# The first norm of a hybrid decoder step, its squares taken from a second load of x and applied within the fourth tile

## The chip, the core and the metric

The kernel runs on one core of one Trainium2 chip. The metric is device time in microseconds (us) for one execution; the times below are medians of three runs, and one further execution was profiled.

## The reference, cut to what matters

One layer of a decoder trunk is computed for 512 prompt tokens and 32 sample tokens (8 sequences of 4). The part concerned is its beginning: the first RMSNorm and the input projection.

```python
def rmsnorm(x, w):
    xf = x.astype(jnp.float32)
    y = xf * lax.rsqrt(jnp.mean(xf * xf, axis=-1, keepdims=True) + EPS)
    return (y * w.astype(jnp.float32)).astype(x.dtype)
...
    h = rmsnorm(x, norm_mix_w)
    proj = h @ w_in
    ...
    xbc = proj[..., o4:o5]
    dt_raw = proj[..., o5:]
    ...
    xbc_c, new_conv_ssd = causal_dwconv(xbc, conv_ssd_prev, conv_ssd_w, conv_ssd_b)
    xbc_c = jax.nn.silu(xbc_c)
    ...
    dt = jax.nn.softplus(dt_raw.astype(f32) + dt_bias.astype(f32))
    ...
    y, ssm_new = ssd_scan(xs, dt, A, Bm, Cm, ssm_prev)
```

x has 2048 columns; `xbc` has 12 tiles of 128 columns (tiles 0 to 7 feed the scan's values, 8 and 9 its B, 10 and 11 its C), dt has 16 columns. Attention, the output projection and the gated MLP follow and take most of the time.

## The kernel before, in words

Activations lie transposed: 128 columns of x on the partitions, the 544 tokens in two halves of 272 (256 prompt, 16 sample). x has 16 such k-tiles. Each fp32 operand is split into a rounded part (`hi`) and a residual (`lo`), and a product is three matmuls, hi·hi, lo·hi and hi·lo (`mm3`, L166 on; every matmul is recorded at L158). The norm's factor `rstd` differs by token only, so the matmuls take x times the norm's weights, and `rstd` is multiplied in where a PSUM tile is read (the evictions at L305 and L306).

The start works as follows. For each k-tile of x (the loop over `k`): SyncE loads `xt` into one of six buffers (L241); for even k the next 256 columns of the weights of tiles 8 and 10 (`FIRST`) are loaded (L149) and split, `whi` by ScalarE (L150) and `wlo` by VectorE (L151), two raw buffers being shared by all weight loads; then x is split, `xh` by VectorE for even k (L251) and by ScalarE for odd k (L253), and `xl` by VectorE (L254). ScalarE squares `xt` (L257, L260); GpSimd, for every fourth k VectorE, adds the squares into `ssq` (L261). TensorE runs the two first tiles over all k together into four PSUM halves (three buffers of the tag `po`, one of `sB`); after the fourteenth k it multiplies `ones` by `ssq` and `rms_rstd` takes root and reciprocal. After these tiles comes dt's projection (`dt_linear`: 64 matmuls whose weights, `wdthi`, are split at L274 and L275). Then the evictions and convolutions of tiles 8 and 10, tiles 0 to 3, the other six tiles, and so on. `conv` evicts two halves, runs three multiply-adds on VectorE (L316) and SiLU on ScalarE.

What sets the order. TensorE's order is the order in which the program is written. On the other engines a scheduler orders the instructions: of those that its model calls ready, the earliest written goes first. Each queue (the five engines and SyncE's DMA queue) then runs strictly in its order. Work that is to be woven between the matmuls of the projections is written as tasks of the class `Side`: `mm3` calls `side.poll()`, and a task goes on when the matmul time since its last step exceeds what it yielded. dt's steps (`dt_stage`), lambda (`lam`) and the two groups of the scan (`ssd`) are such tasks, each starting after the one ahead of it. Weight tiles are loaded and split ahead of need: `plan` queues sources, `wfill(n)` issues splits until n chunks of 1024 columns wait in `wbuf`, and `wnext` fills up to three and takes one; the chunks rotate through three buffers each of `whi` and `wlo`.

Memory is given out in pools stacked by address. The pool `sA` (the buffers `xt`, `ssq`, `sq`, and four `whi` and four `wlo` of 4 KB per partition for the first tiles) is released after the first tiles' matmuls, and `sS` takes the same addresses: `mixy0`, `mixy1` (8.5 KB each), `ctail`, `bc0` to `bc3` (2.1 KB each), then what is asked for next. A tile of `sS` can be written only when the tile of `sA` under it has been read for the last time.

Of the kernel before, what the change touches and what calls it, by code (L numbers as in the profile page):

```python
# [16 lines left out]
P = 128  # L17
# [82 lines left out]
def body(tc, i, o):  # L100
# [32 lines left out]
    def half(tag="po"):  # L133
        return ps.tile([P, 512], F32, name="po", tag=tag, bufs=3 if tag == "po" else 1)
# [60 lines left out]
    def linear(xs, evac, tags=("po", "po")):  # L195

        ch = [wnext(), wnext()]
        for hf in range(2):
            po = half(tags[hf])
            for k in range(NK):  # L200
                mm3(po, kslice(ch, k), xs[k], hf, k == 0, k == NK - 1)
            evac(hf, po)

# [20 lines left out]
    xs = {}  # L224
    ssq = sA.tile([P, 2, HT], F32, name="ssq")
    ssq2 = sA.tile([P, 2, HT], F32, name="ssqb")
    first = [[half(), half()], [half(), half("sB")]]
# [9 lines left out]
    fw = [[], []]  # L237
    sub = 256
    for k in range(NK):
        xt = sA.tile([P, 2, HT], F32, name="xt", tag="xt", bufs=6)  # L240
# [8 lines left out]
        xs[k] = xslot(k)  # L249
        if k % 2 == 0:  # L250
            V.tensor_scalar(xs[k][0], xt, nw_mix[:, k:k + 1], None, op0=ALU.mult)  # L251
        else:
            A.activation(xs[k][0], xt, AF.Copy, scale=nw_mix[:, k:k + 1])  # L253
        V.scalar_tensor_tensor(xs[k][1], xt, nw_mix[:, k:k + 1], rd(xs[k][0]), op0=ALU.mult, op1=ALU.subtract)  # L254
        e, acc = (V, ssq2) if k % 4 == 2 else (G, ssq)
        if k in (0, 2):
            A.activation(acc, xt, AF.Square)  # L257
        else:
            sq = sA.tile([P, 2, HT], F32, name="sq", tag="sq", bufs=3)
            A.activation(sq, xt, AF.Square)  # L260
            e.tensor_tensor(acc, acc, sq, op=ALU.add)  # L261
    k1 = pack(cst, "k1")
    ones, nw_ffn, nw_fin = (k1[n] for n in ("ones", "nw_ffn", "nw_fin"))
    V.tensor_tensor(ssq, ssq, ssq2, op=ALU.add)
    kS = pack(sC, "kS")
# [6 lines left out]
    wdt = kS["w_dt"].rearrange("p (k h) -> p k h", h=SH)  # L272
    whi = sC.tile([P, NK, 2 * SH], FR, name="wdthi")
    A.activation(whi[:, :, 0:SH], wdt, AF.Copy)  # L274
    V.tensor_tensor(whi[:, :, SH:2 * SH], wdt, rd(whi)[:, :, 0:SH], op=ALU.subtract)  # L275
    for k in range(NK):
        for f in range(2):
            for hf in range(2):
                mm3(first[f][hf], kslice(fw[f], k), xs[k], hf, k == 0, k == NK - 1)
        if k == 13:  # L280
            rstd = rms_rstd(cst, ssq, DM, tag="rstd")
    sA.release()
# [5 lines left out]
    ctail = sS.tile([P, NC_X, 27], F32, name="ctail")  # L288
    bc = [sS.tile([P, 2, HT], F32, name=f"bc{j}") for j in range(4)]
    def conv(pool, tg, lin, nw, par, prev, tail, dst, bufs=2):  # L290

# [34 lines left out]
    def xbc(j):  # L326
        dst = mixy[j // 4][:, j % 4] if j < 8 else bc[j - 8]
        evac = conv(sS, "s", LX, CW, cpar[:, j], cprev[:, j], ctail[:, j], dst)
        if j in FIRST:
            for hf in range(2):  # L330
                evac(hf, first[FIRST.index(j)][hf])
        else:
            linear(xs, evac)
# [10 lines left out]
    def dt_stage(po, res):  # L344
        yield 1.5
        dtr = sS.tile([2 * SH, SEQ + NS3], F32, name="dtr", tag="spre", bufs=2)
# [273 lines left out]
    squared = []  # L620
    podt = dt_linear()
    res = []
    t_dt = side.add(dt_stage(podt, res))


# [25 lines left out]

    for j in FIRST:
        xbc(j)
    for j in range(4):
        xbc(j)
# [821 lines left out]
def host_inputs(x):  # L1477
# [5 lines left out]
    xx = np.concatenate([x["x_prompt"].reshape(SEQ, DM), x["x_sample"].reshape(NS, DM)], 0)[perm]  # L1483
    d["xT"] = xx.T.reshape(NK, P, 2, HT)
    w_in = np.asarray(x["w_in"])[0]
    nt = 44
# [123 lines left out]
```

## Time and profile before

| | |
|---|---|
| median of 3 runs | 2421.18 us (2420.86 to 2428.1) |
| profiled execution | 2424.79 us, of which the span of instructions is 2423.0 us |
| TensorE busy | 2349.6 us (97%), 18184 matmuls |
| VectorE busy | 2074.0 us (86%) |
| ScalarE busy | 1140.5 us (47%) |
| GpSimd busy | 677.1 us (28%) |
| DMA moved | 350.44 MB, 145 GB/s in the mean |

In the rows PE is TensorE's matmuls, PEld its weight loads, DVE VectorE, ACT ScalarE, POOL GpSimd, SP SyncE; a q behind an engine is its queue of DMA issues. L150 is a line of the kernel's file. Times are us from the start of the span, durations of one instruction in groups are ns. PEclk is the clock granted to TensorE, 1.00 being 2.4 GHz and 0.50 being 1.2 GHz. An arrow in brackets names what ended an idle time. Busy times of TensorE are modelled from pipelined matmuls, so its pace is better read from the starts of successive matmuls.

### The profile page before, as it was taken

The page shows a single profiled execution, that of the slowest core. Times are in us where ns is not written, and L with a number is a line of the kernel's source. Part 1 is how long each engine was busy: PE and PEld are TensorE (multiplying, and loading weights), DVE is VectorE, ACT ScalarE, POOL GpSimd, SP SyncE. Part 2 cuts the span into 40 slices and gives each one's busy share as a digit, 9 for nine tenths or more (in the row PEclk, how much of TensorE's full clock was granted, in tenths as well). Part 3 has the DMA queues.
Part 4 walks back from the last instruction along what each step waited for, and adds up shares of the span by engine and source line. Part 5 has one row for each costly group of instructions (what it writes and reads, how often), then busy time and mean ns, then how long its engine had stood idle before and what let it go on. Part 6 is the DMA issues. An engine that isn't in the chain of part 4 may idle for free.

```text
span 2423.0 us, 46336 instructions
## 1 busy us (share of the span) xinstructions
PE 2349.6 (97%) x18184; PEld 2299.1 (95%) x18184; DVE 2074.0 (86%) x2925; ACT 1140.5 (47%) x1651; POOL 677.1 (28%) x643
## 2 busy tenths in 40 slices
PE   7999999999999999899999999999999899899997
PEld 7989898998999999899999999999999899899997
DVE  8686778787876556999999999999999988988986
ACT  5645345656565333444444444444444534435345
POOL 4243233333321111233223232322222122222323
PEclk9999999999999999999999999999999999999998
DMA  4434444454544543333434343343433755747432
GB/s 157 139 119 137 154 155 144 143 160 147 164 161 155 167 137 120 120 127 123 137 111 138 119 142 119 128 133 115 139 109 132 228 179 176 228 153 249 124 114 83
DMA packets 172284, 350.44 MB, mean 145 GB/s; under 512 B 19474, under 2 KB 89874, under 8 KB 172066
## 3 DMA queue, kind: packets, MB, share of 16 engines
q1 hardware_dynamic: 168370, 335.51, 43.2%
q0 software_dynamic: 2880, 11.14, 1.3%
q8 instruction: 143, 2.34, 0.4%
q10 hardware_dynamic: 816, 0.84, 0.1%
q14 instruction: 75, 0.61, 0.1%
HBM read 293.07 MB, written 54.35 MB: 143 GB/s over the span
## 4 chain that ended last, share of the span: by engine, by line
PE 61%; DVE 6%; DMA 2%; ACT 1%; issue 1%; SPq 0%; DVEq 0%; ACTq 0%
PE po L158 59%; DVE wlo L1063 1%; DVE wx L1063 1%; DVE xl L1063 1%; DMA st<-hTs 1%; DMA st<-hB 1%; ACT whi L1069 1%; DVE ssq L1467 0%; DMA wraw<-in_w_last 0%; PE pos L158 0%; PE scs L158 0%; DVE acc L316 0%; DVE T2l L1063 0%; DVE y L1449 0%; DMA wraw<-in_w_down 0%
## 5 line engine op out<-in xcount | busy, mean ns | idle before, releaser
L158 PE MATMUL po<-xh,whi 128*128 128x272 f32 x3968 | 1159.8, 292 | 12.7 <-ACT whi L150 5.2
L158 PE MATMUL po<-xh,wlo 128*128 128x272 f32 x3968 | 1151.5, 290 | 6.2 <-DVE wlo L1063 5.0
L158 PE MATMUL po<-xl,whi 128*128 128x272 f32 x3968 | 1149.6, 290 | 6.5 <-DVE xl L254 6.5
L158 PEld LDWEIGHTS po<-xh,whi 128*128 128x128 f32 x3968 | 756.3, 191 | 20.8 <-ACT whi L150 5.2
L158 PEld LDWEIGHTS po<-xh,wlo 128*128 128x128 f32 x3968 | 754.5, 190 | 13.6 <-DVE wlo L1063 6.8
L158 PEld LDWEIGHTS po<-xl,whi 128*128 128x128 f32 x3968 | 754.8, 190 | 7.5 <-DVE xl L254 7.5
L1069 ACT ACTIVATE whi<-wx 128x1024 fp32r<-128x1024 f32 (+2 forms) x340 | 343.3, 1010 | 475.7 <-PE po L158 452.8
L1063 DVE TENSOR_TENSOR wlo<-wx,whi 128x1024 fp32r<-128x1024 f32 (+2 forms) x340 | 429.6, 1264 | 49.3 <-ACT whi L1069 47.0
L151 DVE TENSOR_TENSOR wlo<-wraw,whi 128x1024 fp32r<-128x1024 f32 (+1 forms) x132 | 167.2, 1272 | 61.7 <-ACT whi L150 61.4
L1069 ACT ACTIVATE whi<-wraw 128x1024 fp32r<-128x1024 f32 (+2 forms) x136 | 137.0, 1007 | 173.2 <-PE po L158 168.5
L150 ACT ACTIVATE whi<-wraw 128x1024 fp32r<-128x1024 f32 (+1 forms) x132 | 127.8, 976 | 101.5 <-PE po L158 72.1
L1063 DVE TENSOR_TENSOR wlo<-wraw,whi 128x1024 fp32r<-128x1024 f32 (+2 forms) x136 | 167.8, 1234 | 5.0 <-ACT whi L1069 2.7
L1063 DVE TENSOR_TENSOR wx<-wraw,wx 128x1024 f32<-128x1024 f32 (+2 forms) x136 | 166.2, 1222 | 1.2
L699 POOL TENSOR_TENSOR kvl<-kv,kvh 128x512 fp32r<-128x512 f32 x64 | 104.5, 1634 | 180.4 <-ACT kvh L697 167.3
L158 PE MATMUL po<-T1h,wlo 128*128 128x272 f32 x512 | 148.6, 290 | 5.8 <-DVE wlo L1063 5.8
L158 PE MATMUL po<-T2h,wlo 128*128 128x272 f32 x512 | 148.6, 290 | 5.0 <-DVE wlo L1063 5.0
L158 PE MATMUL po<-T2h,whi 128*128 128x272 f32 x512 | 147.9, 289 | 2.2 <-ACT whi L1069 2.2
L158 PE MATMUL po<-T1h,whi 128*128 128x272 f32 x512 | 147.7, 289 | 1.4 <-ACT whi L1069 1.4
L158 PE MATMUL po<-T2l,whi 128*128 128x272 f32 x512 | 148.1, 289 | 0.0
L158 PE MATMUL po<-T1l,whi 128*128 128x272 f32 x512 | 148.1, 289 | 0.0
L158 PE MATMUL po<-B11h,whi 128*128 128x272 f32 x512 | 147.1, 287 | 0.7 <-DVE u L1139 0.7
L158 PE MATMUL po<-B11h,wlo 128*128 128x272 f32 x512 | 147.6, 288 | 0.0
(408 smaller groups left out, 4155.3 us busy)
## 6 DMA issues: line engine op xcount, KB each, us to landing
wx<-in_w_gu SPq DMA_DIRECT2D x88, 512.0 KB, 3.9
wraw<-in_w_gu SPq DMA_DIRECT2D x88, 512.0 KB, 3.9
wraw<-in_w_in SPq DMA_DIRECT2D x84, 512.0 KB, 3.8
kv<-in_kc SPq DMA_DIRECT2D x128, 128.0 KB, 2.2
kv<-in_vc SPq DMA_DIRECT2D x128, 128.0 KB, 2.8
wraw<-in_w_out SPq DMA_DIRECT2D x32, 512.0 KB, 3.7
wx<-in_w_down SPq DMA_DIRECT2D x32, 448.0 KB, 3.9
wraw<-in_w_down SPq DMA_DIRECT2D x32, 448.0 KB, 3.7
```

Of the source, the lines that this page charges most:

```text
L150: A.activation(hi[:, c], raw[:, c], AF.Copy)
L151: V.tensor_tensor(lo[:, c], raw[:, c], rd(hi[:, c]), op=ALU.subtract)
L158: T.matmul(out, lhsT=lhsT, rhs=rhs, start=start, stop=stop)
L699: e.tensor_tensor(l[:, s], src[:, s], rd(h)[:, s], op=ALU.subtract)
L1063: e.tensor_tensor(out, a, b, op=op)
L1069: A.activation(h, src, AF.Copy)
```

## The change

The squares leave the split loop, with their accumulators and GpSimd's and VectorE's additions; ScalarE now makes all sixteen `xh`. ScalarE's order becomes the written order from the loop to the end of the norm (`manual_schedule`). x is loaded a second time with the tokens on the partitions (`xtp`, `xts`: ten pieces of up to 128 tokens x 1024 columns, 512 KB each but for two of 32 tokens), on ScalarE's own DMA queue, three buffers of the tag `m` in `sS` in turn. ScalarE squares each piece with a sum along the row. The first three issues are written behind the split loop, ahead of dt's weight split; the four PSUM halves of tiles 8 and 10 are copied to `bc` so that their buffers come free. TensorE goes on without the norm: dt, tile 0, the first half of tile 1. There `norm1` takes root and reciprocal by token, spreads them on diagonals (128 x 640) and multiplies with `ones`; then come the second half of tile 1, the evictions and convolutions of 0, 1, 8 and 10 and tiles 2 and 3. dt's task starts behind the norm, its first pause is gone.

```diff
--- before.py
+++ after.py
@@ -196,10 +196,14 @@
 
         ch = [wnext(), wnext()]
         for hf in range(2):
-            po = half(tags[hf])
-            for k in range(NK):
-                mm3(po, kslice(ch, k), xs[k], hf, k == 0, k == NK - 1)
-            evac(hf, po)
+            evac(hf, linear_half(ch, hf, tags[hf], xs))
+
+    def linear_half(ch, hf, tag, x=None):
+        x = x or xs
+        po = half(tag)
+        for k in range(NK):
+            mm3(po, kslice(ch, k), x[k], hf, k == 0, k == NK - 1)
+        return po
 
     def xslot(k):
         return [xsp.tile([P, 2, HT], FR, name=f"x{n}{k}", tag=f"x{n}{k}") for n in "hl"]
@@ -222,8 +226,6 @@
     sC = tc.alloc_tile_pool(name="sC", bufs=1)
     sA = tc.alloc_tile_pool(name="sA", bufs=1)
     xs = {}
-    ssq = sA.tile([P, 2, HT], F32, name="ssq")
-    ssq2 = sA.tile([P, 2, HT], F32, name="ssqb")
     first = [[half(), half()], [half(), half("sB")]]
     for j in list(range(4)) + [9, 11, 4, 5, 6, 7]:
         plan(i["w_in"][32 + j])
@@ -236,6 +238,8 @@
         plan(i["w_in"][28 + j])
     fw = [[], []]
     sub = 256
+    act = contextlib.ExitStack()
+    act.enter_context(tc.manual_schedule(engines={mybir.EngineType.Activation}))
     for k in range(NK):
         xt = sA.tile([P, 2, HT], F32, name="xt", tag="xt", bufs=6)
         dma(out=xt, in_=i["xT"][k])
@@ -247,21 +251,10 @@
             for c in ch:
                 c[2]((k % 8) // 2)
         xs[k] = xslot(k)
-        if k % 2 == 0:
-            V.tensor_scalar(xs[k][0], xt, nw_mix[:, k:k + 1], None, op0=ALU.mult)
-        else:
-            A.activation(xs[k][0], xt, AF.Copy, scale=nw_mix[:, k:k + 1])
+        A.activation(xs[k][0], xt, AF.Copy, scale=nw_mix[:, k:k + 1])
         V.scalar_tensor_tensor(xs[k][1], xt, nw_mix[:, k:k + 1], rd(xs[k][0]), op0=ALU.mult, op1=ALU.subtract)
-        e, acc = (V, ssq2) if k % 4 == 2 else (G, ssq)
-        if k in (0, 2):
-            A.activation(acc, xt, AF.Square)
-        else:
-            sq = sA.tile([P, 2, HT], F32, name="sq", tag="sq", bufs=3)
-            A.activation(sq, xt, AF.Square)
-            e.tensor_tensor(acc, acc, sq, op=ALU.add)
     k1 = pack(cst, "k1")
     ones, nw_ffn, nw_fin = (k1[n] for n in ("ones", "nw_ffn", "nw_fin"))
-    V.tensor_tensor(ssq, ssq, ssq2, op=ALU.add)
     kS = pack(sC, "kS")
     kT.update(pack(sK, "kT"))
     ident, nssd = kT["ident"], kT["nw_ssd"]
@@ -270,15 +263,10 @@
     dtb, alog, dsk, maskT, tri, tri32, blk32, mask32, bmask, ii, ii32 = (
         kS[n] for n in ("dt_bias", "a_log", "d_skip", "maskT", "tri", "tri32", "blk32", "mask32", "bmask", "ii", "ii32"))
     wdt = kS["w_dt"].rearrange("p (k h) -> p k h", h=SH)
-    whi = sC.tile([P, NK, 2 * SH], FR, name="wdthi")
-    A.activation(whi[:, :, 0:SH], wdt, AF.Copy)
-    V.tensor_tensor(whi[:, :, SH:2 * SH], wdt, rd(whi)[:, :, 0:SH], op=ALU.subtract)
     for k in range(NK):
         for f in range(2):
             for hf in range(2):
                 mm3(first[f][hf], kslice(fw[f], k), xs[k], hf, k == 0, k == NK - 1)
-        if k == 13:
-            rstd = rms_rstd(cst, ssq, DM, tag="rstd")
     sA.release()
 
 
@@ -287,6 +275,57 @@
     mixy = [sS.tile([P, 4, 2, HT], F32, name=f"mixy{g}") for g in range(2)]
     ctail = sS.tile([P, NC_X, 27], F32, name="ctail")
     bc = [sS.tile([P, 2, HT], F32, name=f"bc{j}") for j in range(4)]
+
+
+    ss = sS.tile([P, 5, 2], F32, name="ss")
+    xqs = []
+
+    def sq_load():
+        c, n = divmod(len(xqs), 2)
+        rows = P if c < 4 else NS
+        t = sS.tile([P, 1024], F32, name="xq", tag="m", bufs=3)[:rows]
+        A.dma_start(out=t, in_=i["xtp"][c, :, n] if c < 4 else i["xts"][:, n])
+        xqs.append((t, ss[:rows, c, n:n + 1]))
+
+    def sq_sum(n):
+        t, acc = xqs[n]
+        A.activation(t, t, AF.Square, accum_out=acc)
+        if n < 7:
+            sq_load()
+
+    for n in range(3):
+        sq_load()
+    whi = sC.tile([P, NK, 2 * SH], FR, name="wdthi")
+    A.activation(whi[:, :, 0:SH], wdt, AF.Copy)
+    V.tensor_tensor(whi[:, :, SH:2 * SH], wdt, rd(whi)[:, :, 0:SH], op=ALU.subtract)
+    V.memset(ss[:, 4], 1.0)
+    sq_sum(0)
+    wfill(1)
+    for f in range(2):
+        for hf in range(2):
+            A.activation(bc[FIRST[f] - 8][:, hf], first[f][hf][:, 0:HT], AF.Copy)
+    for n in range(1, 4):
+        sq_sum(n)
+        wfill(min(n + 1, 3))
+    for n in range(4, 8):
+        sq_sum(n)
+    rstd = cst.tile([P, 2, HT], F32, name="rstd", tag="rstd")
+
+    def norm1():
+
+        r = sS.tile([P, 5], F32, name="rcol")
+        V.tensor_tensor(r, ss[:, :, 0], ss[:, :, 1], op=ALU.add)
+        A.activation(r, r, AF.Sqrt, scale=1.0 / DM, bias=epsc)
+        V.reciprocal(r, r)
+        dg = sS.tile([P, 5, P], F32, name="rdiag", tag="m", bufs=3)
+        V.tensor_tensor(dg, ident.unsqueeze(1).broadcast_to([P, 5, P]), r.unsqueeze(2).broadcast_to([P, 5, P]), op=ALU.mult)
+        for hf in range(2):
+            pt = ps.tile([P, 512], F32, name="pn", tag=("sA", "pb")[hf])
+            for c in range(2):
+                mm(pt[:, c * P:(c + 1) * P], ones, dg[:, 2 * hf + c])
+            mm(pt[:, HP:HT], ones[:NS], dg[:NS, 4, hf * HS:(hf + 1) * HS])
+            A.activation(rstd[:, hf], pt[:, 0:HT], AF.Copy)
+
     def conv(pool, tg, lin, nw, par, prev, tail, dst, bufs=2):
 
 
@@ -328,7 +367,13 @@
         evac = conv(sS, "s", LX, CW, cpar[:, j], cprev[:, j], ctail[:, j], dst)
         if j in FIRST:
             for hf in range(2):
-                evac(hf, first[FIRST.index(j)][hf])
+                evac(hf, dst[:, hf])
+        elif j == 0:
+            for hf in range(2):
+                evac(hf, held[hf])
+        elif j == 1:
+            evac(0, held[2])
+            evac(1, linear_half(ch1, 1, "po"))
         else:
             linear(xs, evac)
 
@@ -342,7 +387,7 @@
         return po
 
     def dt_stage(po, res):
-        yield 1.5
+        yield 0.0
         dtr = sS.tile([2 * SH, SEQ + NS3], F32, name="dtr", tag="spre", bufs=2)
         V.tensor_tensor(dtr[:, 0:SEQ].rearrange("p (a t) -> p a t", a=2), pro(po)[:2 * SH], pro(rstd)[:2 * SH], op=ALU.mult)
         V.tensor_tensor(dtr[:, SEQ:TOK].rearrange("p (a t) -> p a t", a=2), smp(po)[:2 * SH], smp(rstd)[:2 * SH], op=ALU.mult)
@@ -619,8 +664,18 @@
 
     squared = []
     podt = dt_linear()
+    held = []
+    linear(xs, lambda hf, po: held.append(po))
+    for n in range(8, 10):
+        sq_sum(n)
+    ch1 = [wbuf.pop(0), wbuf.pop(0)]
+    held.append(linear_half(ch1, 0, "po"))
+    norm1()
+    act.close()
     res = []
     t_dt = side.add(dt_stage(podt, res))
+    side.poll()
+    side.poll()
 
 
     cosr, sinr = (kT[n].rearrange("p (a t) -> p a t", a=2) for n in ("cos", "sin"))
@@ -649,9 +704,7 @@
 
     t_lam = side.add(lam(), t_dt)
 
-    for j in FIRST:
-        xbc(j)
-    for j in range(4):
+    for j in (0, 1) + FIRST + (2, 3):
         xbc(j)
     t0 = side.add(ssd(res, 0), t_lam)
     for j in (9, 11, 4, 5, 6, 7):
@@ -1482,6 +1535,8 @@
     d = {}
     xx = np.concatenate([x["x_prompt"].reshape(SEQ, DM), x["x_sample"].reshape(NS, DM)], 0)[perm]
     d["xT"] = xx.T.reshape(NK, P, 2, HT)
+    d["xtp"] = np.asarray(x["x_prompt"]).reshape(4, P, 2, DM // 2)
+    d["xts"] = np.asarray(x["x_sample"]).reshape(NS, 2, DM // 2)
     w_in = np.asarray(x["w_in"])[0]
     nt = 44
     d["w_in"] = w_in[:, :nt * P].reshape(NK, P, nt, P).transpose(2, 1, 0, 3).reshape(nt, P, DM)
```

## Rows read from the trace of the kernel before

**Rows 1.** Part 1 of the page: busy us, share of the span, number of instructions
```profile
PE 2349.6 (97%) x18184; PEld 2299.1 (95%) x18184; DVE 2074.0 (86%) x2925; ACT 1140.5 (47%) x1651; POOL 677.1 (28%) x643
```

**Rows 2.** Stretches: length, busy of PE, PEld, DVE, ACT, POOL, then PEclk, DMA share, GB/s
```profile
10.00:40.00 30.00, 23.21 (x144) 22.16 (x145) 29.96 (x38) 18.64 (x35) 15.79 (x10) 0.91 0.60 198
15.00:20.00 5.00, 2.51 (x18) 2.02 (x16) 5.00 (x5) 2.41 (x5) 4.22 (x3) 1.00 0.20 56
25.00:35.00 10.00, 9.37 (x74) 9.02 (x73) 9.96 (x14) 7.88 (x16) 5.39 (x3) 1.00 0.98 335
37.50:41.50 4.00, 4.00 (x20) 4.00 (x21) 4.00 (x8) 0.25 (x1) 0.00 (x0) 0.57 0.36 98
46.00:100.00 54.00, 54.00 (x429) 51.92 (x428) 37.91 (x88) 30.78 (x54) 18.85 (x27) 1.00 0.41 126
540.00:544.00 4.00, 3.65 (x29) 3.65 (x30) 3.96 (x9) 1.25 (x3) 1.90 (x1) 1.00 0.84 237
```

**Rows 3.** TensorE in order of time: start, duration, instruction, [idle before it]
```profile
41.91 1.19 PE L158 MATMUL pn<-ssq,k 128*128 128x272 f32 x4
...
45.55 0.29 PE L158 MATMUL po<-xh,whi 128*128 128x272 f32 x1
...
45.80 0.28 PE L158 MATMUL po<-xl,whi 128*128 128x272 f32 x1
...
540.35 0.38 PE L158 MATMUL sc<-ka,qa 128*128 128x256 f32 x1 [2.40 <-ACT p L784]
```

**Rows 4.** TensorE's waits up to 46 us: us in total, times, longest
```profile
PE po L158 <- DVE xl L254: 6.5, 4, 1.8
PE po L158 <- ACT whi L150: 5.2, 1, 5.2
PE po L158 <- DVE wlo L151: 1.1, 2, 0.9
```

**Rows 5.** Groups up to 46 us: busy us, mean ns, idle before them
```profile
L261 POOL TENSOR_TENSOR ssq<-ssq,sq 128x544 f32<-128x544 f32 x11 | 17.1, 1557 | 18.9 <-ACT sq L260 18.4
L254 DVE SCALAR_TENSOR_TENSOR xl<-xt,k,xh 128x544 fp32r<-128x544 f32 x16 | 15.3, 982 | 0.1
...
L150 ACT ACTIVATE whi<-wraw 128x256 fp32r<-128x256 f32 x16 | 6.2, 411 | 3.4 <-DMA wraw<-in_w_in 3.4
L253 ACT ACTIVATE xh<-xt,k 128x544 fp32r<-128x544 f32 x8 | 5.9, 742 | 4.5 <-DMA xt<-in_xT 4.5
...
L150 ACT ACTIVATE whi<-wraw 128x1024 fp32r<-128x1024 f32 x2 | 2.0, 1047 | 0.0
```

**Rows 6.** VectorE in order of time
```profile
4.82 0.78 DVE L254 SCALAR_TENSOR_TENSOR xl<-xt,k,xh 128x544 fp32r<-128x544 f32 x1
...
47.03 0.41 DVE L305 TENSOR_TENSOR pre<-po,rstd 128x256 f32<-128x256 f32 x1
47.36 0.17 DVE L306 TENSOR_TENSOR pre<-po,rstd 128x16 f32<-128x16 f32 x1
...
55.97 0.67 DVE L347 TENSOR_TENSOR dtr<-podt,rstd 32x512 f32<-32x512 f32 x1
```

**Rows 7.** ScalarE in order of time, at the start and near the end
```profile
6.06 0.42 ACT L150 ACTIVATE whi<-wraw 128x256 fp32r<-128x256 f32 x1 [0.89 <-DMA wraw<-in_w_in]
...
2386.66 1.28 ACT L1443 ACT_TABLE_LOAD   x1
2387.95 0.49 ACT L1443 ACTIVATE st<-pn,k 128x272 f32<-128x272 f32 x1
```

**Rows 8.** DMA issues up to 46 us: KB each, median us from issue to landing
```profile
wraw<-in_w_in SPq DMA_DIRECT2D x2, 512.0 KB, 4.2
kT<-in_kT SPq DMA_DIRECT2D x1, 764.5 KB, 7.2
```

**Rows 9.** Line L1450, the DMA issues on ScalarE's queue: ns min/median/max
```profile
L1450 ACTq DMA_DIRECT2D out_yT<-y x3: 379/379/427, 2414.1 to 2417.8; - x3
```

**Rows 10.** Line L784, reading ScalarE's accumulator: ns min/median/max
```profile
L784 ACT ACTIVATION_READ_ACCUMULATOR p<-sc,mx x64: 185/195/207, 336.1 to 724.6; 128x1 f32 x64
```

## The prediction, made before the change was run

> **What bounds the kernel now.** I read the page's totals first: TensorE is busy for 97% of the span, VectorE for 86% [rows 1]. An average over stages does not tell where a change at the start pays, so next I read stretches. From 46 to 100 us TensorE is busy in all 54 us at a granted clock of 1.00; from 10 to 40 us only in 23.2 of 30, at 0.91 [rows 2]. So what can be won lies in the first 46 us. There the first two weight tiles are 192 matmuls of 272 columns (16 k-tiles x 2 tiles x 2 halves x 3 terms), the last of them at 45.80 us; at the full-rate pace (0.125 us from 45.55 to 45.80 in two steps [rows 3]) they would take 24 us. The list of waits says where the rest goes: 5.2 us until the first split is there, 6.5 us in four waits for `xl` and 1.1 for `wlo` [rows 4]. The remaining 8 us or so are low clock and overlap: in the 4 us behind one of those waits the granted clock was 0.57, that is mostly 1.2 GHz instead of 2.4, and 20 matmuls ran in place of 32 [rows 2].
>
> Why is `xl` late? VectorE is busy in 29.96 of the 30 us from 10 to 40 [rows 2], but its instructions are stretched: the residual of x takes 0.78 us at 4.82, before GpSimd works, and 0.98 in the mean of 16, while GpSimd adds squares for 17.1 us [rows 5, 6]. Late `xl` also holds the six `xt` buffers and the two raw weight buffers, and the loads behind them: from 15 to 20 us the DMA share is 0.20 [rows 2].
>
> **Part 1, the split loop.** Gone are GpSimd's 11 additions, VectorE's 8 `xh` and its additions, and ScalarE's 16 squares. Left are, on VectorE, 16 x 0.78 for `xl` and 16 x 0.41 for `wlo` (at ScalarE's price for the same piece) = 19 us in 30; on ScalarE 16 x 0.74 for `xh` and 16 x 0.41 for the pieces = 18.4 us [rows 5, 6]. The loads are 16 x 272 KB and 16 x 128 KB, 6.6 MB, which at the 335 GB/s of the stretch from 25 to 35 us [rows 2] are 20 us. Each is less than TensorE's 24, so TensorE binds, if nothing holds the loads.
>
> It starts later. ScalarE's written order puts both weight pieces ahead of `xh0`; the second was split only at 6.06 us, behind its DMA [rows 7]. So `xh0` is ready at 6.06 + 0.42 + 0.74 = 7.2, in place of the 5.2 us wait [rows 4]. From 7.2 I let 4 us go at the low clock, 20 matmuls as in that stretch [rows 2]; 172 x 0.125 = 21.5 us more end at 32.7. The weights' second half must wait for the raw buffers: the last pieces in them are split at about 14 us, a load takes 4.2 [rows 8], so the next `xl` stands at about 21, when TensorE gets there too. I add 0.8 us for that: the stage ends at T = 33.5. The bounds are 32.5, where no load is late, and 45, where nothing is won.
>
> **Part 2, dt's weights behind the loads.** ScalarE's next instructions are three DMA issues into pool `sS`, then dt's split. By the pools' sizes in the code (in `sA` 13 KB of `xt`, then eight weight buffers of 4 KB; in `sS` some 27 KB ahead of `xq`) the first `xq` lies over the fourth `whi` buffer, which the stage's last matmul reads. All of it therefore waits for T, in ScalarE's order, where dt's split was ready early before. TensorE gets a gap: three issues of 0.38 [rows 9] (0.46 with handover), the split 0.41 and VectorE's residual 0.41 = 2.4 us with the semaphores between; bounds 2.0 and 3.0. Does a gap of this length cost clock? Behind the `xl` wait of at most 1.8 us it did (0.57), behind one of 2.40 us at 540 it did not (1.00) [rows 2 to 4]. I take the first, which is nearest in stage and matmuls: 4 x 0.43 = 1.7 us.
>
> **Part 3, the norm.** Ten squares (the two of 32 rows are as wide) are 1.05 us each, as any 1024-wide ACTIVATE, plus 0.20 to read the accumulator [rows 5, 10]; ScalarE also has four weight splits of 1.05, four PSUM copies at about 0.45 and seven issues at 0.46. From T + 4.4, when the first load has landed (4.2 [rows 8]), that is 12.5 + 4.2 + 1.8 + 3.2 = 21.7: T + 26.1 if no later load is late. Table load and Sqrt (1.3 + 0.2), the reciprocal and the 640-wide product (0.8, an estimate between `xl`'s 544 and a 1024-wide split) bring the norm's operand to T + 29. TensorE gets there at T + 2.4 + 1.7 + 8.0 (dt's 64 at 0.125) + 12.0 + 6.0 = T + 30.1. One late load eats this; I take a wait of 0.5 (0 to 3). The new products have 544 columns, as many as the old four, which took 1.2 us [rows 3]: 1.1.
>
> In the row the Sqrt starts 1.29 us behind its table load's start at 2386.66 [rows 7]. The Trainium skill (ScalarE: Activation LUTs, What ACT_TABLE_LOAD costs) puts a drain of some 1.4 us on top, 2.66 us in all; by that page the norm would come at T + 30.4 and the sum would be some 0.3 us worse. The row decides.
>
> Then all three `po` buffers hold halves that wait for `rstd`, so TensorE stops until one is evicted: `rstd`'s copy 0.45, dt's product 0.67 and two short ones 0.35, the eviction 0.41 + 0.16 [rows 6], overlapped 2.2 us; 1.2 if the eviction goes ahead of dt. The clock costs 1.7 again.
>
> **Part 4, what moves.** The evictions, convolutions and dt's chain of what was tiles 8, 10, 0 and half of 1 now begin at the norm; the matmuls of the rest of tile 1 and of tile 2 (18 us) are their cover, and without it they are the second rival. The scan of group 0 starts some 6 us later (the pauses written in dt's and lambda's tasks are 32 us, now from a point 18 us of matmuls later). That moves its own waits: 0, with 4 us to either side, from stops of the length in [rows 3] and their clock. GpSimd's copies and rotary products move along, off the path; SyncE's weight loads keep their order, and ScalarE's seven issues are in the sum.
>
> **Sum.** 33.5 + 2.4 + 1.7 + 0.5 + 1.1 + 2.2 + 1.7 = 43.1 us for what ended at 45.9, the norm included both times: 2.8 us won. The profiled execution took 2424.79 us, 3.6 above the median of 2421.18; against the median that is 2418. A measurement of this kernel can tell about 0.3%, 7.3 us, from no change.
>
> **The rivals.**
> *Short waits* (faster). The 2.40 us gap that cost no clock [rows 2, 3] may be the rule here: T = 32.7, the norm hidden, the eviction first, no loss: 32.7 + 2.4 + 1.1 + 1.2 = 37.4, 8.5 won, about 2412.5; with the scan's 4 us 2409. For it: ScalarE and VectorE have room in Part 1. Against: one such row stands against the low clock in the first stage.
> *VectorE's queue behind the norm* (slower). From 46 to 100 us VectorE was busy 37.9 us [rows 2]; some 20 of them now wait for the norm, and then stand ahead of the weight residuals of tile 2, which the program asks for after them, since `ch1` is taken without a refill. Tile 2 needs its second pair about 10 us behind the restart. If the 20 us must be worked off first, TensorE waits 10 us: 2.8 won become 7 lost, 2428; with a stretch as in `xl` (0.98 for 0.78 [rows 5, 6]) 12 lost. From a wait of 2.8 us on nothing is left. Against: dt's chain of short dependent steps leaves gaps for residuals.
> *Late loads.* A 764 KB load took 7.2 us where 512 KB alone took 4.2 [rows 8]. If three at once take 7.2 each, the three rounds over the buffers cost 3 us more each and the norm is some 8 us late: about 6 lost, 2427. Against: 4.4 MB and three weight chunks in 25 us are 240 GB/s, and 335 was moved [rows 2].
> The Trainium skill (DMA: Bandwidth & Descriptors, Issuing engines are not separate DMA queues) says that transfers of all queues interleave on the same 16 engines; by it the second load of x, though on ScalarE's queue, takes its time from the weights.
> *Nothing won.* If x's transfers bind the first stage, T stays near 43 and the two new waits come on top: 7 lost, 2428. Against: the share of 0.20 while buffers were held [rows 2].
>
> **How the numbers follow.** The sum as worked out 0.47, short waits 0.29, VectorE's queue 0.14, late loads and nothing won 0.05 each. Faster by over 7.3 us is most of the short waits, 0.26. Slower by as much is 0.09 of VectorE's queue and 0.04 of the last two, 0.13. Within it is the rest, 0.61. The range goes from the short waits with the scan's gain, 2409, to the late loads, 2427; the likeliest case's own is 2414 to 2422.
>
> **What would show it.** `xl` at 0.78 us throughout and the 192nd matmul at 32 to 35 us; then a gap of 2 to 3 us put down to dt's residual, with a low granted clock behind it; a second gap behind the `pn` matmuls, put down to an eviction. If the stage ends past 38 us, if no gap stands ahead of dt, or if waits for `wlo` of over 3 us stand in tile 2, that step is wrong.

## The result, and the profile after

The changed kernel takes 2439.14 us in the median of 4 runs (2437.0 to 2443.39), the kernel before, on the same chip, 2422.57 us: a ratio of 1.0067 with a 95% interval of 1.0054 to 1.0079. It is slower by some 16.5 us where 2.8 us were to be won, above the range, whose upper end was 2427. The profiled execution of after took 2440.18 us (span 2438.4), 15.4 us more than that of before.

The totals answer to [rows 1]: TensorE is busy for 10.7 us longer with 8 matmuls more, VectorE for 20 us less.

```profile
PE 2360.3 (97%) x18192; PEld 2310.1 (95%) x18192; DVE 2054.0 (84%) x2915; ACT 1145.5 (47%) x1665; POOL 660.5 (27%) x632
```

The stretches answer to [rows 2]: length, busy time of PE, PEld, DVE, ACT and POOL, then granted clock, DMA share and GB/s.

```profile
15.00:20.00 5.00, 5.00 (x42) 5.00 (x42) 3.57 (x8) 3.37 (x7) 0.00 (x0) 1.00 0.92 253
...
34.00:46.00 12.00, 10.49 (x72) 8.84 (x73) 2.87 (x3) 7.01 (x14) 0.00 (x0) 0.86 0.66 228
...
46.00:100.00 54.00, 44.91 (x319) 43.64 (x317) 28.31 (x71) 28.18 (x42) 11.17 (x23) 0.91 0.33 111
60.00:70.00 10.00, 6.57 (x30) 6.12 (x28) 3.63 (x5) 6.70 (x10) 0.00 (x0) 0.66 0.31 108
70.00:80.00 10.00, 7.88 (x49) 7.37 (x49) 4.89 (x14) 2.05 (x4) 3.27 (x9) 0.83 0.00 0
...
80.00:96.00 16.00, 16.00 (x130) 16.00 (x129) 14.56 (x41) 11.95 (x18) 6.76 (x14) 1.00 0.18 67
...
100.00:110.00 10.00, 7.90 (x33) 6.39 (x34) 3.74 (x14) 2.88 (x8) 0.39 (x2) 0.52 0.14 54
```

The first stage is cured: from 15 to 20 us TensorE is busy throughout (before: half of the time), and loads move at 253 GB/s in place of 56. But from 34 to 46 us VectorE has only 2.87 us of work, and from 80 to 96 it is nearly full. Behind that, from 100 to 110 us, TensorE does 33 matmuls at a clock of 0.52.

TensorE in order of time, its stops up to 110 us (start, duration, instruction, idle before it); the second row is the last of the 192 matmuls of the first tiles:

```profile
6.37 0.59 PE L158 MATMUL po<-xh,whi 128*128 128x272 f32 x1 [6.37 <-ACT xh L254]
...
32.87 0.28 PE L158 MATMUL po<-xl,whi 128*128 128x272 f32 x1
35.51 0.58 PE L158 MATMUL podt<-xh,wdthi 128*32 128x272 f32 x2 [2.36 <-DVE wdthi L300]
...
62.82 0.51 PE L158 MATMUL po<-xh,whi 128*128 128x272 f32 x1 [2.68 <-ACT whi L150]
...
64.08 0.59 PE L158 MATMUL po<-xh,wlo 128*128 128x272 f32 x1 [0.75 <-DVE wlo L151]
...
69.46 2.04 PE L158 MATMUL pn<-rdiag,k 128*128 128x128 f32 x12
...
73.62 0.57 PE L158 MATMUL po<-xh,whi 128*128 128x272 f32 x1 [2.12 <-DVE pre L345]
...
102.10 0.69 PE L158 MATMUL pc<-dta,kS 128*128 128x64 f32 x2 [5.65 <-DVE dta L429]
```

The last of the 192 starts at 32.87 us where before had it at 45.80 [rows 3]: 12.9 us won. Then come stops of 2.36, 2.68, 0.75, 2.12 and 5.65 us, 13.6 in all, where before had none from 46 to 110 us. After four of them (not the 0.75) the clock is low: 0.86, 0.66, 0.83 and 0.52 in the stretches above. From 60 to 110 us TensorE is busy for 38.81 us with 240 matmuls; before needed 50.00 us for 398, so 240 are worth 30.2, and some 8.6 us are low clock. The stretch from 60 to 110 us, before and after, columns as above:

```profile
60.00:110.00 50.00, 50.00 (x398) 49.13 (x398) 31.43 (x72) 33.51 (x60) 10.78 (x14) 1.00 0.49 152
60.00:110.00 50.00, 38.81 (x240) 36.10 (x239) 30.82 (x83) 25.52 (x41) 11.56 (x25) 0.80 0.18 64
```

With 1.7 us of low clock (12 x 0.14) from 34 to 46, that is about 24 us lost by 110 us. The first product of the second scan group (`px`) stands behind the same number of the projections' matmuls in both kernels. It starts 14.7 us later, before and after:

```profile
220.62 0.60 PE L163 MATMUL px<-kT,mixy 128*128 128x128 f32 x4
235.28 0.60 PE L163 MATMUL px<-kT,mixy 128*128 128x128 f32 x4
```

27.6 us have gone since the 192nd matmul, 24 of them accounted for here; most of the rest is the stretch from 170 to 235 us, with a stop of 3.62 us in place of 0.61 and 2.39, and a clock of 0.92 for 0.95. The norm's own matmuls, which before had ahead of its 192nd, are another 1 us at full pace.

Who is late shows on ScalarE in order of time. Its order is the written one:

```profile
33.19 1.35 ACTq L287 DMA_DIRECT2D xq<-in_xtp  x3
34.58 0.42 ACT L299 ACTIVATE wdthi<-kS 128x256 fp32r<-128x256 f32 x1 [7.81 <-issue]
...
43.21 1.05 ACT L292 ACTIVATE xq<-xq 128x1024 f32<-128x1024 f32 x1
...
49.93 1.06 ACT L150 ACTIVATE whi<-wraw 128x1024 fp32r<-128x1024 f32 x1 [5.59 <-DMA wraw<-in_w_in]
...
60.68 1.06 ACT L292 ACTIVATE xq<-xq 128x1024 f32<-128x1024 f32 x1 [3.96 <-DMA xq<-in_xtp]
...
61.73 1.04 ACT L150 ACTIVATE whi<-wraw 128x1024 fp32r<-128x1024 f32 x1
...
65.81 1.28 ACT L318 ACT_TABLE_LOAD   x1
67.11 0.30 ACT L318 ACTIVATE rcol<-rcol,k 128x5 f32<-128x5 f32 x1
```

The third weight chunk waits 5.59 us for its load, and squares whose data lie there wait behind it; a later square waits 3.96 us for x, and the fourth chunk, which TensorE needs, waits behind that until 61.73. Two streams of loads share one queue of instructions, and each lateness is handed on to the other. The Sqrt starts 1.30 us behind its table load's start, as in [rows 7]. The drain that the Trainium skill adds there (ScalarE: Activation LUTs, What ACT_TABLE_LOAD costs) is not seen.

VectorE in order of time shows dt's chain from its first operand to the last of its results, `dta`:

```profile
79.79 0.22 DVE L402 TENSOR_TENSOR dtx<-pd,kS 128x64 f32<-128x64 f32 x1
...
88.45 0.19 DVE L420 TENSOR_SCALAR dtp<-dtp 128x80 f32<-128x80 f32 x1
88.57 0.81 DVE L355 SCALAR_TENSOR_TENSOR acc<-pre,kS,acc 128x568 f32<-128x568 f32 x1
89.30 0.24 DVE L419 TENSOR_TENSOR dtp<-dtp,dts 128x80 f32<-128x80 f32 x1
89.45 0.80 DVE L355 SCALAR_TENSOR_TENSOR acc<-pre,kS,acc 128x568 f32<-128x568 f32 x1
...
101.82 0.23 DVE L429 SCALAR_TENSOR_TENSOR dta<-dt,ea 128x80 f32<-128x80 f32 x1
```

Each small step of 0.2 us stands in turn with a convolution's 0.8 us (or an eviction, or a weight residual of 1.2). The chain takes 22.0 us; before it took 13.7:

```profile
59.71 0.22 DVE L357 TENSOR_TENSOR dtx<-pd,kS 128x64 f32<-128x64 f32 x1 [2.40 <-PE pd L158]
...
73.38 0.24 DVE L384 SCALAR_TENSOR_TENSOR dta<-dt,ea 128x80 f32<-128x80 f32 x1
```

dt's task writes the cumulative sums (`pc`) 18 us of matmuls behind its first step (pauses of 2 and 16), and TensorE stands there.

### The profile page after: what moved, and what is told of

The parts are those of the page before. It is cut to its first block, busy times and chain, and to the rows that moved or that the text cites. A ratio compares the mean times of both kernels' runs of the same rounds, so it can differ in the third digit from the quotient of the medians.

```text
span 2438.4 us, 46346 instructions
## 1 busy us (share of the span) xinstructions
PE 2360.3 (97%) x18192; PEld 2310.1 (95%) x18192; DVE 2054.0 (84%) x2915; ACT 1145.5 (47%) x1665; POOL 660.5 (27%) x632
## 4 chain that ended last, share of the span: by engine, by line
PE 57%; DVE 5%; DMA 2%; ACT 1%; issue 1%; SPq 0%; DVEq 0%; ACTq 0%
PE po L158 57%; DVE wlo L1116 1%; DMA st<-hB 1%; DVE xl L1116 1%; DVE wx L1116 1%; DMA st<-hTs 1%; ACT whi L1122 0%; DVE ssq L1520 0%; DMA wraw<-in_w_last 0%; DVE acc L355 0%; DVE y L1502 0%; ACT u L1518 0%; DVE x L1513 0%; DMA x<-x1d 0%; DVE st L1497 0%
## 5 line engine op out<-in xcount | busy, mean ns | idle before, releaser
L151 DVE TENSOR_TENSOR wlo<-wraw,whi 128x1024 fp32r<-128x1024 f32 (+1 forms) x132 | 158.9, 1207 | 86.9 <-ACT whi L150 86.6
```

The costliest lines, as they stand in the source:

```text
L151: V.tensor_tensor(lo[:, c], raw[:, c], rd(hi[:, c]), op=ALU.subtract)
```

## The experiments

Each batch ran beside the kernel before, whose medians were 2423.26 (e1 to e4), 2422.06 (e6 to e9), 2423.87 (e5, e10) and 2424.0 us (e11, e12).

### The four waits, one by one (e1 to e4)

e1 puts 10 us more between dt's chain and its sums:

```diff
-        yield 16.0
+        yield 26.0
         pc = ps.tile([P, 8, 64], F32, name="pc", tag="sA")
```

> The changed kernel with one number altered: dt's task pauses 26 instead of 16 us of matmul time before its cumulative-sum matmuls (pc). Theory A: the changed kernel loses most behind the norm because VectorE's chain for dt stands between four convolutions and comes 5.65 us late for matmuls whose place in TensorE's order is fixed, with half-rate clock behind the stop. Then the wait of pc for dta falls from 5.65 us to under 1, the low clock behind it goes, and the time falls by 6 to 10 us, to about 2430. Rival B: VectorE is simply behind by that much, and the next thing that needs it (the tile's evictions or weight residuals) stops TensorE in its place. Then pc no longer waits, but the time stays within 3 us of 2439. Rival C: the scan starts 10 us later and is not done when the gate asks for it: slower than 2442.

Measured: 2438.7 us, ratio 1.0058 [1.0043, 1.0073]. The stop at `pc` is gone, and the second group's `px` comes at 228.92 in place of 235.28. But what was won is given back at a new stop, where TensorE waits for a buffer that VectorE frees late, as rival B had it:

```profile
321.74 0.57 PE L158 MATMUL po<-xh,whi 128*128 128x272 f32 x1 [6.21 <-DVE q L761]
```

e2 puts the splits of the third and fourth weight chunk behind the squares of the prompt:

```diff
-    wfill(min(n + 1, 3))
+    wfill(min(n + 1, 2))
 for n in range(4, 8):
     sq_sum(n)
+wfill(3)
```

The squares are numbered from 0: the last line stands behind number 7, the last of those with 128 rows.

> The changed kernel with the third weight chunk split behind the seventh square instead of between the third and the fourth. Theory A: ScalarE, in its written order, stood 5.6 us before that split for a weight load, the squares behind it, so the norm was late and so was the fourth chunk's split, for which TensorE stopped 2.68 + 0.75 us. Then the 5.6 us go, the last square ends near 57 instead of 64.7 us, TensorE's stop for whi in tile 1 goes with the low clock behind it, and the time falls by 4 to 6 us. Rival: ten loads of 512 KB and the weights share the DMA engines, so the squares' own loads set the end; then the last square stays past 61 us and the time stays within 2 us.

Measured: 2432.99 us, 1.0037 [1.0023, 1.005]. The stop for `whi` shrinks to 0.2 us, `pn` comes at 65.39 in place of 69.46, the stops behind it stay (2.12, and 4.64 at `pc`). By the medians, ScalarE's written order cost about 6 us. Two things do not fit so well: the last square ends at 61.0 us in place of 64.8, where the theory had 57, and the profiled execution, at 2439.24 us the slowest of six, does not show where the 6 us lie.

e3 splits dt's weights ahead of the three loads:

```diff
-    for n in range(3):
-        sq_load()
     whi = sC.tile([P, NK, 2 * SH], FR, name="wdthi")
...
+    for n in range(3):
+        sq_load()
```

> The changed kernel with dt's weight split written ahead of the three loads of x instead of behind them; nothing else. Theory: the 2.36 us stop at 35.5 us is ScalarE's in-order queue, where the loads wait for the last matmul that reads the buffer under them. Then podt follows the first tiles without a stop, the granted clock stays at 1.00, and the time falls by about 4 us (2.4 of stop, 1.5 of clock). Rival: the loads then start no earlier, the norm is no earlier, and what is won in front is waited for behind, at tile 1's weights and the norm: then the podt stop is gone but the time falls by less than 1.5 us.

Measured: 2438.02 us, 1.0064 [1.0051, 1.0077]. The gap ahead of dt is gone, and TensorE reaches tile 1 earlier, to wait there 6.6 us for `whi` in place of 2.7: the rival is right. As long as the weights are late, a gap ahead of them is free.

e4 gives the second half of tile 1 a free PSUM buffer:

```diff
-            evac(1, linear_half(ch1, 1, "po"))
+            evac(1, linear_half(ch1, 1, "sB"))
```

> The changed kernel with the second half of tile 1 accumulated in the PSUM buffer sB instead of po, so that it need not wait for an eviction behind the norm; nothing else. Theory: the 2.12 us stop behind pn goes and the time falls by 2 to 4 us (with the clock). Rival: TensorE then reaches the pc matmuls 2 us sooner and waits there that much longer for dta: the stop behind pn goes, that at pc grows from 5.65 to 7.5 us or more, and the time stays within 1.5 us.

Measured: 2430.55 us, 1.0031 [1.0019, 1.0043]: 8.6 us less than after, more than expected. The stop behind `pn` is gone, that at `pc` is 3.86; in the profiled execution the stop for `whi` is 0.7 us, though nothing was done about it. That stop varies from one execution to the next (0.7 here, 2.68 in after, 2.92 in e9, all with the same order up to there). The profiled execution took 2435.7 us, 5 more than the median, so the trace does not show where the whole gain comes from.

### Part 1 alone, and the additions (e6, e7)

e6 is the kernel before with ScalarE making all `xh`; it leaves out the squares of 15 of 16 k-tiles and their additions.

> The kernel before, with Part 1 of the change alone: ScalarE makes all sixteen xh; the squares and their additions are left out but for the first k-tile's, so that the norm's sum leaves out 15 of 16 k-tiles. The norm stays where it was. Theory (the split loop's relief is worth what Part 1 said, and the change lost it again behind the norm): the 192nd matmul at 32 to 35 us, nothing new later, 2409 to 2413. Rival (what is won at the start is waited for later whatever the change adds, since VectorE's work for the convolutions and dt is bunched behind it): the 192nd matmul as early, but stops of 5 us or more between 46 and 350 us that the kernel before lacks, 2418 to 2424.

Measured: 2412.24 us, 0.996 [0.9947, 0.9974]. dt's first matmul starts at 34.08 (45.92 before), and of those 11.8 us 12.3 are there at the first `sc`, attention's first product (315.91 for 328.21). No stop of 5 us or more comes between there and 350 us. The theory holds: Part 1 is worth what it said, if nothing is moved behind it; of the 12.3 us, 9.8 are left in the median of the whole kernel.

e7 is the kernel before with its eleven GpSimd additions on VectorE:

```diff
-        e, acc = (V, ssq2) if k % 4 == 2 else (G, ssq)
+        e, acc = V, (ssq2 if k % 4 == 2 else ssq)
```

> The kernel before with all additions of squares on VectorE, none on GpSimd. Theory (GpSimd's additions stretch VectorE's xl): the mean of xl goes from 0.98 to about 0.80 us, but VectorE takes over 11 additions of some 0.65 us, 7 us against 3 us saved, so the first stage gets 2 to 5 us longer: 2424 to 2428. Rival (xl is stretched by its own load or by ScalarE): xl stays at 0.95 to 1.0 us, and the stage gets 7 us longer, 2429 to 2432.

Measured: 2430.33 us, 1.0037 [1.0023, 1.005]. The groups up to 48 us, against 982 ns in [rows 5]:

```profile
L254 DVE SCALAR_TENSOR_TENSOR xl<-xt,k,xh 128x544 fp32r<-128x544 f32 x16 | 12.1, 793 | 0.0
...
L261 DVE TENSOR_TENSOR ssq<-ssq,sq 128x544 f32<-128x544 f32 x11 | 8.1, 734 | 0.0
...
L151 DVE TENSOR_TENSOR wlo<-wraw,whi 128x256 fp32r<-128x256 f32 x16 | 6.1, 430 | 0.0
L251 DVE TENSOR_SCALAR xh<-xt,k 128x544 fp32r<-128x544 f32 x8 | 4.1, 511 | 5.6 <-DMA xt<-in_xT 5.6
```

The last two of these groups in the kernel before, up to 46 us:

```profile
L151 DVE TENSOR_TENSOR wlo<-wraw,whi 128x256 fp32r<-128x256 f32 x16 | 11.8, 775 | 0.6 <-ACT whi L150 0.6
L251 DVE TENSOR_SCALAR xh<-xt,k 128x544 fp32r<-128x544 f32 x8 | 7.2, 902 | 6.1 <-DMA xt<-in_xT 6.1
```

`xl` is as short as the theory said, so the additions on GpSimd did stretch it. But the stage did not get longer: dt's first matmul comes at 41.24, 4.7 us sooner, though VectorE has 8.1 us more to do. Neither expectation saw that `wlo` and `xh` were stretched too: with `xl` they fall from 34.3 to 22.3 us, by more than the additions bring. The loss comes later, in part in a stop of 4.25 us for a weight split at 53.60; the profiled execution, 2426.1 us, is the shortest of five, so the trace does not show all of it. The time lies in the rival's range, but not for the rival's reason.

### dt's chain away from VectorE (e9, e8, e10)

e9 is after with dt's polynomial on GpSimd (L416 to L424, `V.` changed to `G.`):

```diff
-            V.tensor_tensor(pl, pl, s2, op=ALU.mult)
-            V.tensor_scalar(pl, pl, 2.0 / d, None, op0=ALU.add)
+            G.tensor_tensor(pl, pl, s2, op=ALU.mult)
+            G.tensor_scalar(pl, pl, 2.0 / d, None, op0=ALU.add)
```

> The changed kernel with dt's polynomial (21 small operations of 128 x 80) on GpSimd in place of VectorE, nothing else. Theory (the operand of dt's cumulative sums is late because the chain stands in turn with convolution operations of 0.8 us in VectorE's queue): the chain takes under 15 us in place of 22, the stop of 5.65 us at pc is under 1 us, 2430 to 2434. Rival (the stop is only where TensorE meets a backlog of VectorE): the stop at pc goes, but one of 4 us or more stands elsewhere before 350 us, as with the longer pause, and the time is 2436 to 2441.

Measured: 2436.98 us, 1.0059 [1.0046, 1.0073], the rival's time, with a stop of 3.93 us elsewhere. The chain takes 16.9 us, not under 15. VectorE in order of time, where it takes up dt's chain again:

```profile
97.21 0.25 DVE L429 SCALAR_TENSOR_TENSOR dta<-dt,ea 128x80 f32<-128x80 f32 x1 [6.35 <-POOL dt L424]
...
97.88 1.21 DVE L151 TENSOR_TENSOR wlo<-wraw,whi 128x1024 fp32r<-128x1024 f32 x1
```

And TensorE, which wanted that residual:

```profile
99.15 0.59 PE L158 MATMUL po<-xh,wlo 128*128 128x272 f32 x1 [3.93 <-DVE wlo L151]
```

The chain ends 4.6 us sooner, but VectorE itself now waits for GpSimd, with a weight residual behind it in its queue, and the stop moves to that residual. The second rival of the prediction had named a residual as the waiter, though one of tile 2; this is the first of tile 3.

e8 joins e2, e3, e4 and e9.

> The changed kernel with dt's weight split ahead of the three loads, the third and fourth weight chunks' splits behind the seventh square, tile 1's second half in the buffer sB, and dt's polynomial (21 small operations) on GpSimd. Theory (four separate waits, each of which cost TensorE its length and a stretch of low clock): no stop over 1 us between 8 and 105 us, gains that add up, 2439 - 8.6 - 6 - 5 - 1 = 2418, and the gain stays to the end. Rival (the backlog of VectorE only shows elsewhere): the stops move to the first scan group, behind px or pys, and the time stays at 2425 to 2430.

Measured: 2429.39 us, 1.0024 [1.0008, 1.0039]: the rival's time, but not its stop. The sum of single gains (2418) isn't reached; the largest stop is again 4.67 us for a residual at 90.14, behind VectorE's wait of 6.82 us for GpSimd.

e10 is e8 with `dta` and `am` on GpSimd as well:

```diff
-        V.scalar_tensor_tensor(a, dt, -1.0, ea.unsqueeze(1).broadcast_to(n_), op0=ALU.mult, op1=ALU.mult)
+        G.tensor_scalar(ea, ea, -1.0, None, op0=ALU.mult)
+        G.tensor_tensor(a, dt, ea.unsqueeze(1).broadcast_to(n_), op=ALU.mult)
```

> As the run with all four parts, but the last two operations of dt's chain (dta and am) are on GpSimd too, so that VectorE never waits for GpSimd. There VectorE stood 6.82 us for GpSimd's dt, and TensorE behind it 4.67 us for a weight residual. Theory (that stop was made by the order of VectorE's queue, not by the amount of its work): no stop over 1 us between 8 and 170 us, and 4.7 us plus some 1.5 us of low clock less: 2421 to 2424. Rival (VectorE's work behind the norm is too much in any order): a stop of 3 us or more for wlo or for the first scan group's inputs, 2427 to 2431.

Measured: 2428.4 us, 1.0013 [1.0003, 1.0024]. The stop for the residual is gone (0.9 at most), as the theory had it; in this execution 3.62 us stand again for `whi` at 58.67, 1.04 at `pc`, and 3.57 in the first scan group at 180.78, where before had 0.61 and 2.39. The time is the rival's, but the stop for `whi` is none that either named.

e5 joins e1 to e4, with the chain on VectorE.

> The changed kernel with dt's weight split first, the weight chunks' splits behind the squares, tile 1's second half in sB, and the longer pause of 10 us in dt's task; the chain stays on VectorE. Theory (with VectorE's queue relieved of nothing, the pause only moves the stop): no stop at pc, but one of 4 to 6 us at 310 to 330 us for q, as with the pause alone: 2426 to 2430. Rival (the stop at q came of the start's loss of 14 us, not of the pause): no stop over 2 us up to 350 us, 2418 to 2423.

Measured: 2430.71 us, 1.0025 [1.0016, 1.0034], 0.7 above the theory's range. No stop at `pc`, 4.27 us for `whi` at 59.11, and 6.18 us at 314.24 for `q`: that stop belongs to the longer pause, as the theory said, not to the loss at the start.

### The order alone (e12)

e12 is the kernel before, squares and place of the norm included, with the change's order of tiles: the four halves copied to `bc`, then dt, tile 0, half of tile 1, and only then dt's task and the evictions.

```diff
+    held = []
+    linear(xs, lambda hf, po: held.append(po))
+    ch1 = [wbuf.pop(0), wbuf.pop(0)]
+    held.append(linear_half(ch1, 0, "po"))
...
-    for j in FIRST:
-        xbc(j)
-    for j in range(4):
+    for j in (0, 1) + FIRST + (2, 3):
         xbc(j)
```

> The kernel before with the change's order of tiles alone: split loop, squares and the place of the norm's matmuls as before, but the halves of tiles 8 and 10 copied to bc, then dt, tile 0, half of tile 1, and only then dt's task and the evictions of 0, 1, 8 and 10 in the written order. rstd is there early. Theory (the harm is that the norm sets free some 20 us of VectorE's work at once): with rstd early the evictions spread, the stop at pc is under 2 us, 2421 to 2426. Rival (the order itself does it: dt's chain stands between convolutions that were half done before it): a stop of 4 us or more at pc or for a weight residual between 80 and 120 us, 2427 to 2434.

Measured: 2431.5 us, 1.003 [1.002, 1.0039]: 7.5 us lost with nothing of the norm changed, in the rival's range, though in the profiled execution (2428.9 us, the shortest of nine) the stop at `pc` is 2.12 us and not 4. TensorE in order of time, where it waits:

```profile
95.34 0.44 PE L158 MATMUL pc<-dta,kS 128*128 128x64 f32 x2 [2.12 <-DVE dta L397]
```

The stretches around it, columns as above:

```profile
90.00:100.00 10.00, 7.88 (x53) 6.63 (x51) 8.32 (x23) 4.93 (x9) 1.80 (x6) 0.88 0.30 107
100.00:110.00 10.00, 10.00 (x66) 9.62 (x65) 1.69 (x5) 1.66 (x6) 2.40 (x1) 0.78 0.56 134
```

The chain runs from 75.42 to 95.05, 19.6 us. The stop and the low clock behind it (10 x 0.12 + 10 x 0.22 = 3.4 us) are 5.5, and the scan's stop at `pys` is 4.10 where before had 0.61 and 2.39. At the second group's `px` it is 7.6 us behind (228.22).

### The squares summed by TensorE (e11)

e6 and e12 together say: keep the relief of the split loop, and the order of before. e11 does so without a second load: ScalarE rounds the squares to the matmuls' format, TensorE multiplies ones by them.

```diff
+    oner = sA.tile([P, P], FR, name="oner")
...
-        e, acc = (V, ssq2) if k % 4 == 2 else (G, ssq)
...
+        sq = sA.tile([P, 2, HT], FR, name="sq", tag="sq", bufs=4)
+        A.activation(sq, xt, AF.Square)
+        sqs.append(sq)
...
+    def sumsq(k):
+        for hf in range(2):
+            mm(pn[hf][:, 0:HT], oner, sqs[k][:, hf], k == 0, k == NK - 1)
```

> The kernel before, its order of tiles and its place of the norm nearly kept, but the squares are rounded to the matmuls' format by ScalarE and added up by TensorE (32 matmuls of ones with a square, one k-tile behind the first tiles' own), so that GpSimd's and VectorE's additions are gone; there is no second load of x. Theory (what the change won at the start came of taking the additions away from GpSimd and VectorE, and needs no move of the norm): xl at 0.78 to 0.80 us, the first tiles and the sums done at 36 to 39 us in place of 45.9, nothing new later, 2413 to 2417. Rival (root and two reciprocals of 1.8 us now stand behind the last sum, and TensorE waits for rstd behind dt's 8 us; or ScalarE's 23 us of work hold xl): stops of 2 to 5 us up to 60 us, 2418 to 2423.

Measured: 2415.09 us, 0.9959 [0.9942, 0.9975], in the theory's range: 8.9 us below before, and faster than both kernels. TensorE in order of time, at the end of the stage and at the second scan group:

```profile
34.88 0.67 PE L158 MATMUL pn<-sq,oner 128*128 128x272 f32 x4
35.39 0.41 PE L158 MATMUL podt<-xh,wdthi 128*32 128x272 f32 x2
...
209.95 0.60 PE L163 MATMUL px<-kT,mixy 128*128 128x128 f32 x4
```

The stretch that answers to the first of [rows 2]:

```profile
10.00:40.00 30.00, 30.00 (x243) 29.39 (x242) 23.38 (x41) 22.14 (x40) 0.92 (x5) 1.00 0.66 227
```

The group of `xl` up to 46 us:

```profile
L257 DVE SCALAR_TENSOR_TENSOR xl<-xt,k,xh 128x544 fp32r<-128x544 f32 x16 | 12.4, 782 | 2.4 <-ACT xh L256 2.3
```

dt starts 10.5 us sooner than before, and 10.7 are still there at `px`. The 32 added matmuls cost their own 4 us and no stop; root and two reciprocals of 1.8 us end behind them, under dt's matmuls.

## Why the prediction was wrong

**Part 1 was right.** `xl` takes 782 ns in the mean (0.78 foretold), the 192nd matmul starts at 32.87 us (33.5), and e6 keeps the gain to the end.

**Part 2 was right**: 2.36 us (2.4), and 1.7 us of clock (1.7) behind it. That ScalarE's loads take their time from the weights' is in the trace too, as the Trainium skill has it (DMA: Bandwidth & Descriptors, Issuing engines are not separate DMA queues): a 512 KB weight load landed after 5.3 us in the median up to 70 us, 4.2 in [rows 8].

**Part 3 failed in "I take a wait of 0.5 (0 to 3)".** The norm's own operand was in time (`pn` has no stop ahead of it), but only since TensorE was late itself, 3.4 us for the fourth chunk's split and residual, at half pace behind them. I had counted ScalarE's work, not what each instruction in its written order may wait for. By the medians of e2 that is worth 6 us. The stop at the eviction, 2.12 us (2.2), was right; its clock cost was 1.4 us (1.7), for 13 matmuls start 0.23 us apart in place of 0.125. By e4 its removal brought more than both.

**Part 4 is the larger step that failed.** It costed the bunched work at nothing: "the matmuls of the rest of tile 1 and of tile 2 (18 us) are their cover". The work behind the norm is a chain as well as a sum. 18 us cover a chain of 13.7, not one of 22, which is what it takes when it stands in turn with the bunched convolutions. TensorE stopped 5.65 us at `pc` and then ran at half pace until 110.7 us. e12 prices the order alone at 7.5 us, with the norm early. Part 3's miss or this one, each by itself, takes back more than the 2.8 us that the sum had won.

**The sum.** Behind the first stage it had 9.6 us (43.1 less 33.5); the trace has 27.6. The 18 us between are the stop of Part 3 (3.4 for 0.5), the stop at `pc` (5.65 for nothing), the low clock from 60 to 110 us (8.6 for 1.7) and the scan (some 2.6 for nothing).

**The rivals.** *VectorE's queue behind the norm* was the mechanism, at a chance of 0.14, and its time of 2428 was too small, since Part 3's loss came on top. I had the waiter wrong: the weight residuals of tile 2 were in time, and dt's sums waited. e9 shows that dt's sums and a residual stand in for each other: take the chain out of the queue, and the first residual of tile 3 is late. "Dt's chain of short dependent steps leaves gaps for residuals" spoke against it; the gaps are there, but filled by convolutions, at the chain's expense. *Late loads* happened in a milder form (5.59 and 3.96 us on ScalarE), with the price in the weights, not in the norm. *Short waits* and *nothing won* did not happen: every stop of 2 us or more up to 110 us had a low clock behind it, and the stage ended at 33.

What stays open: the four waits were not fully separable. With all of them attacked (e10) the changed kernel is still 3 to 4.5 us behind before (by the ratio or the medians), so what Part 1 brings is lost there too. From dt's first matmul to the second group's `px`, columns as above, first before and then e10:

```profile
45.92:220.62 174.70, 171.13 (x1330) 161.99 (x1328) 121.63 (x219) 93.10 (x162) 60.64 (x78) 0.98 0.42 127
33.85:225.70 191.85, 180.18 (x1342) 168.16 (x1339) 119.79 (x199) 107.10 (x190) 69.30 (x102) 0.95 0.46 139
```

e10 needs 17.2 us more for the same matmuls of the projections. TensorE stands idle for 11.7 us in place of 3.6, the lower clock is worth some 6 us (191.85 x 0.05 less 174.70 x 0.02), and the norm's matmuls 1; 2 us are not accounted for. One of the stops, 3.62 us for a weight split, varies between executions (0.86 in e8, with the same order up to there). No run holds the evictions back and keeps dt's chain at 13.7 us, so which share of e12's 7.5 us is the chain's is argued from its stop and the clock behind it, not shown by itself.

## What to carry to other kernels

When work is held back and set free together, don't compare its sum with the matmuls beside it: take the longest dependent chain in it, and give each of its steps one of the other instructions as company in the queue. When an engine's order is written out by hand, ask of each instruction which transfer it may wait for, and who stands behind it. And where a relief and a move come in one change, try the relief alone: here it was worth 9 to 10 us, and the move cost more than that.

## What the runs showed of the hardware that was not expected

- GpSimd's additions slowed VectorE beside them, and cost more than they took off it: with the eleven of them moved from GpSimd to VectorE (e7), `xl` fell from 982 to 793 ns, `wlo` from 775 to 430, `xh` from 902 to 511 and an addition from 1557 to 734, and the stage became 4.7 us shorter with VectorE doing all of it.
- These small operations gain nothing on GpSimd (e9): of 128 x 80 elements, a multiplication by a tensor took 0.36 us in the undisturbed part of the chain against 0.23 on VectorE, an addition of a constant 0.41 against 0.19. The chain was shorter although each of its steps was longer: in GpSimd's queue almost nothing stood between them.
- A square of 32 rows x 1024 columns took ScalarE 1.04 us, one of 128 rows 1.06; reading the accumulator 0.18.
- Not every stop cost clock. Behind one of 0.39 us at 45.91 (e10) the granted clock was 1.00 from 46 to 58 us; behind those of 2.12 to 2.36 us in after it was 0.83 and 0.86.
